# Other banks, another order of subtractions, and accumulating transfers in a hybrid decoder layer

## The chip, the cores and the metric

One core of a Trainium2 chip runs the whole layer. The metric is the device time of one execution in microseconds (us); the median of three runs of the kernel before is 1123.79 us. A difference under 0.2% (some 2.2 us) can hardly be told from none.

## The reference

One decoder layer, 256 tokens of width 2048, all in float32:

```python
h   = RMSNorm_pre(x)
p   = h @ W_in                       # 2048 x 5376
A   = sliding_window_attention(p)    # 16 heads, window 128, ALiBi, sinks
R   = hgrn2_recurrence(p)            # 8 heads of 128, chunkwise
m   = concat[RMSNorm(A), R] @ W_out  # 2048 x 2048
x   = x + RMSNorm_post(m)
u   = relu(RMSNorm_pre2(x) @ W_up)   # 2048 x 8192
x   = x + RMSNorm_post2((u * u) @ W_down)
```

The change lies wholly in the last part, from the residual after `W_out` to the end of `W_up` and `W_down`.

## The kernel before

Every large product is made of three matmuls on float32r operands: a weight tile is cast to a high part `whi` on ScalarE (line 90, or 689), the low part `wlo` is subtracted from it on VectorE (line 91, or 694, `split_weight` or `lo_t`), and activations are split in the same way after a TensorE transpose (`turn_act`, lines 637 to 640, `turn_u`, lines 669 to 674). TensorE then adds high by high, high by low and low by high into a PSUM bank of 128 x 512. All weights stream from HBM once, in tiles of 1 MB (128 partitions x 4 x 512).

From the last part of `W_out` on, the order of TensorE, and from the residual of the first token block on also that of VectorE, ScalarE and SyncE, is the order in which the code is written (two manual schedules). GpSimd is not in them; its instructions stand in the order in which their work comes up.

PSUM banks are taken from tags: `sc` has three, `pj` three, `tr` one and `o` one. A transpose into a tag waits until the bank that it takes over has been read, by ScalarE for the high part and by VectorE for the low part.

**The opening of the MLP** (us 397 to 440 of the span): while TensorE ends the second token block of `W_out` (`w3`), VectorE scales the first block's rows (`scaled(tb, c)`, line 704, writing `hn`), TensorE turns them (`turn(tb, c)`), and the first weight tiles of `W_up` are cast and subtracted: `cast2(i)` makes the high part of tile `i` in two halves, `lo_t(i, h)` the low half `h`, and after the second half of tile `i` it issues the load of tile `i + 3`, since three raw tiles fit (tag `raw`). So `lo_t(0, 1)` lets tile 3 load, and `lo2(1)` (both halves of tile 1) lets tile 4 load. `part(tb, tile, "hh" or "lh" or "hl")` are four matmuls each. `residual(tb)` forms the residual and the row statistics of a token block.

**The chunks.** The 8192 columns go in eight chunks of 1024. Chunk 0 is done plainly; chunks 1 to 7 of `W_up` use Winograd's form of Strassen's scheme, with seven products (`m1` to `m7`) instead of eight on sums of quarter tiles. The sums of activations (`turn_sum`, keys `s1` to `s4`) are made once. Sums of weights are made in every chunk by VectorE (`plus`, `add`, line 873), in place on the raw tiles: `X` (upper left), `P` and `Q` (right), and `R`, the lower left tile, which is loaded into a `P` buffer. Each is two 1 MB halves. `X` becomes in turn X+P, X+P+Q, and X+P+Q+R in the end, which `m4` uses; a further sum waits until the split of the earlier one has read the tile.

A period `ch` runs as a list of segments `q`, in which products of chunk `ch` (12 matmuls each half) alternate with `W_down` products of chunk `ch - 1` (24 matmuls each); the list `plan` says at which segment a weight sum is added, `loads` at which one a load is issued, `turns` at which one activations are turned. For each segment the loop runs the sums (`adds`), the split of the weights two segments ahead (`prepare(k + 2)`, three `whi`/`wlo` buffers), then `turns`, the matmuls, and the loads. In the first period (`ch == 1`), segment 1 first turns the activation sum `s4` in two pieces (`turn_sum`, `c` = 0 and 1) and one piece of chunk 0's `u`, segment 2 another piece of `u` (`t(d, 1, 1, d)`). Two of the three `sc` banks hold `W_down` sums at that time.

Of the kernel before, what the change touches and what calls it, by code (L numbers as in the profile page):

```python
# [12 lines left out]
ALU = mybir.AluOpType  # L13
# [16 lines left out]
def tile_hybrid_layer(  # L30
# [17 lines left out]
    nc = tc.nc  # L48
# [4 lines left out]
    w_up_v = w_up[0].rearrange("(kt p) c -> p kt c", p=P)  # L53
# [17 lines left out]
    def bank(tag, bufs=3):  # L71
        return psum.tile([P, 512], F32, tag=tag, name=nm(tag), bufs=bufs)
# [24 lines left out]
    def load_wide(wv, kt0, c0, pieces=1):  # L97
        return [split_weight(wv[:, kt0 + 4 * i:kt0 + 4 * i + 4, c0:c0 + 512], pieces=pieces) for i in range(4)]
# [216 lines left out]
    for tb in range(2):  # L315
        for par in range(2):
            nc.scalar.activation(out=kz[:, par::2, tb, par * HD:(par + 1) * HD],
                                 in_=kvb[tb][:, 0:P].rearrange("p (n d) -> p n d", n=2), func=AF.Copy,
# [323 lines left out]
    def turn(tb, c):  # L642
        turn_act(hn[tb][:, c * 512:(c + 1) * 512], *(h2T[c][:, :, i, tb * P:(tb + 1) * P] for i in range(2)))

    for c in range(3):
        ch = load_wide(w_out_v, 0, c * 512)
# [19 lines left out]
    def turn_u(uT, cb, tb, u, tag, bufs):  # L666
        tp = bank(tag, bufs)
        for i in range(4):
            nc.tensor.transpose(tp[:, i * P:(i + 1) * P], u[:, i * P:(i + 1) * P], ident)  # L669
        u2 = upool.tile([P, 4, P], F32, tag="u2", name=nm("u2"), bufs=2)  # L670
        nc.scalar.activation(out=u2, in_=tp.rearrange("p (a t) -> p a t", a=4), func=AF.Square)
        hi, lo = (uT[cb][:, :, i, tb * P:(tb + 1) * P] for i in range(2))
        nc.scalar.copy(out=hi, in_=u2)
        nc.vector.tensor_tensor(out=lo, in0=u2, in1=hi.bitcast(F32), op=ALU.subtract)
# [16 lines left out]
    def lo_t(i, h):  # L691
        k = slice(2 * h, 2 * h + 2)
        hi, lo = up_w[i]
        nc.vector.tensor_tensor(out=lo[:, k], in0=up_raw[i][:, k], in1=hi[:, k].bitcast(F32), op=ALU.subtract)
        if h == 1:
            load_t(i + 3)
# [5 lines left out]
    def scaled(tb, c):  # L702
        cs = slice(c * 512, (c + 1) * 512)
        nc.vector.scalar_tensor_tensor(out=hn[tb][:, cs], in0=x2[tb][:, cs], scalar=rh[:, tb:tb + 1], in1=gpre[c],
                                       op0=ALU.mult, op1=ALU.mult)

    ch = load_wide(w_out_v, 0, 3 * 512, pieces=2)
# [18 lines left out]
    def part(tb, tile, kind):  # L726
        for kt in range(4 * tile, 4 * tile + 4):
            a = tok(h2T, kt, tb)[1 if kind == "lh" else 0]
            b = up_w[tile][1 if kind == "hl" else 0][:, kt % 4, :]
            nc.tensor.matmul(ps[tb], lhsT=a, rhs=b, start=kt == 0 and kind == "hh", stop=kt == NKT - 1 and kind == "hl")  # L730

    def cast2(i):
        cast_t(i, 0)
        cast_t(i, 1)

    def lo2(i):
        lo_t(i, 0)
        lo_t(i, 1)


    w3(0, 11)
    scaled(0, 0)
    scaled(0, 1)
    cast2(0)
    turn(0, 0)
    scaled(0, 2)
    w3(11, 13)
    turn(0, 1)
    cast2(1)
    scaled(0, 3)  # L750
    lo_t(0, 0)
    w3(13, 15)
    turn(0, 2)
    w3(15, 16)
    turn(0, 3)
    evac_post(3, 1, banks[1])
    lo_t(0, 1)
    cast2(2)
    uT = new_uT()
    ps += [bank("pj"), bank("pj")]  # L760
# [9 lines left out]
    scaled(1, 1)  # L770
    part(0, 0, "hl")
    part(0, 3, "hh")
    turn(1, 0)
    part(0, 3, "lh")
    scaled(1, 2)
# [3 lines left out]
    turn(1, 2)  # L779
    part(1, 1, "hh")  # L780
    turn(1, 3)
    lo2(1)
    part(1, 2, "hh")
    part(1, 3, "hh")
    for tile_ in range(4):
# [11 lines left out]
    def half(tb, h):  # L797
        return hn[tb][:, h * 1024:(h + 1) * 1024]
# [4 lines left out]
    def turn_sum(src, c, tag="sc", bufs=3):  # L803
        t = sums[src[0]]
        turn_act(src[1][:, c * 512:(c + 1) * 512], *(t(slice(4 * c, 4 * c + 4), i) for i in range(2)), tag, bufs)
# [135 lines left out]
    raws, banks3, us, uTs = {}, {}, {0: prev}, {0: uT}  # L941
# [45 lines left out]
        m1[1].act.append(lambda: copy_out(0, "a", ch))  # L987
        return m1

    def t(ch, cb, tb, dst, tag="sc"):  # L990
        return lambda: turn_u(uTs[dst], cb, tb, us[ch][cb, tb], tag, 3)

    def period(ch, m1_next):
        d = ch - 1
        m5 = [up_seg("X", ch, h, "b", lambda: sums["s1"], True) for h in range(2)]
        m6 = [up_seg("X", ch, h, "a", lambda: sums["s2"], False) for h in range(2)]
        m7 = [up_seg("P", ch, h, "a", lambda: sums["s3"], False) for h in range(2)]
        m3 = [up_seg("Q", ch, h, "b", lambda: sums["s4"], False) for h in range(2)]
        m4 = [up_seg("X", ch, h, "a", lambda: sums["a22"], False) for h in range(2)]
        m2 = [up_seg("R", ch, h, "c", lambda: sums["a12"], True) for h in range(2)]  # L1000
        dn = [[down_seg(d, c, h) for h in range(2)] for c in range(4)]
        if ch == 1:
            q = [None, m1_first[0], m1_first[1], dn[0][1], m5[0], m5[1], dn[1][0], m6[0], m6[1], dn[1][1],
                 m7[0], m7[1], dn[2][0], m3[0], m3[1], dn[2][1], m4[0], m4[1], m2[0], m2[1],
                 m1_next[0], dn[3][0], m1_next[1], dn[3][1]]
        else:
            q = [m5[0], m5[1], dn[0][0], m6[0], m6[1], dn[0][1], m7[0], m7[1], dn[1][0], m3[0], m3[1], dn[1][1],
                 m4[0], m4[1], dn[2][0], m2[0], m2[1], dn[2][1], m1_next[0], dn[3][0], m1_next[1], dn[3][1]]
        A, B, C = ((lambda b=b: banks3[b, ch]) for b in "abc")
        m5[1].act.append(lambda: copy_out(1, "b", ch))  # L1010
        m6[1].act.append(lambda: copy_out(2, "a", ch))
        m7[1].dve.append(comb(ch, (1, 1), ALU.subtract, lambda: scr[1], A))
        m7[1].act.append(relu_in_place(ch, (1, 1)))
        m3[1].dve.append(comb(ch, (1, 0), ALU.subtract, B, lambda: scr[2]))
        m3[1].act.append(relu_in_place(ch, (1, 0)))
        m4[1].act.append(lambda: relu_21(ch))
        m2[1].dve.append(comb(ch, (0, 0), ALU.add, C, lambda: scr[0]))
        m2[1].act.append(relu_in_place(ch, (0, 0)))

        def plus(to, frm, c, h):  # L1020
            return lambda: add(raws[to, c, h], raws[frm, c, h])

        nx = ch + 1


        if ch == 1:
            plan = [(1, "X", "P", ch, 0), (2, "X", "P", ch, 1), (3, "X", "Q", ch, 0), (4, "X", "Q", ch, 1),
                    (6, "P", "Q", ch, 0), (7, "P", "Q", ch, 1), (12, "X", "R", ch, 0), (14, "X", "R", ch, 1),
                    (19, "X", "P", nx, 0), (21, "P", "Q", nx, 0), (22, "X", "P", nx, 1), (23, "X", "Q", nx, 0)]
        else:  # L1030
            plan = [(1, "X", "Q", ch, 1), (2, "P", "Q", ch, 1), (8, "X", "R", ch, 0), (10, "X", "R", ch, 1)]
            if nx < NCH:
                plan += [(17, "X", "P", nx, 0), (19, "P", "Q", nx, 0), (20, "X", "P", nx, 1), (21, "X", "Q", nx, 0)]
        for k, to, frm, c, h in plan:
            q[k].adds.append(plus(to, frm, c, h))
        if ch == 1:
            q[1].turns += [lambda c=c: turn_sum(("s4", half(0, 0)), c) for c in range(2)]
            q[1].turns.append(t(d, 1, 0, d))
            q[2].turns.append(t(d, 1, 1, d))
            loads = [(1, "d", d, 1, 1), (4, "d", d, 2, 0), (7, "d", d, 2, 1),  # L1040
                     (8, "R", ch, 0), (9, "R", ch, 1), (10, "d", d, 3, 0), (11, "Q", nx, 0), (12, "Q", nx, 1),
                     (13, "d", d, 3, 1), (14, "X", nx, 0), (15, "X", nx, 1), (16, "P", nx, 0), (17, "P", nx, 1),
                     (19, "d", ch, 0, 0), (21, "d", ch, 0, 1)]
        else:
            q[0].turns += [t(d, 0, 0, d), t(d, 0, 1, d)]
            q[3].turns.append(t(d, 1, 0, d))
            q[4].turns.append(t(d, 1, 1, d))
            loads = [(0, "d", d, 1, 0), (3, "d", d, 1, 1), (5, "R", ch, 0), (6, "R", ch, 1), (6, "d", d, 2, 0),
                     (9, "d", d, 2, 1), (12, "d", d, 3, 0), (15, "d", d, 3, 1),
                     (17, "d", ch, 0, 0), (19, "d", ch, 0, 1)]  # L1050
            if nx < NCH:
                loads += [(8, "Q", nx, 0), (9, "Q", nx, 1), (11, "X", nx, 0), (12, "X", nx, 1), (14, "P", nx, 0),
                          (15, "P", nx, 1)]
        for k, name, *where in sorted(loads, key=lambda x: (x[0], x[1] == "d")):
            q[k].loads.append(lambda name=name, where=where: (load_down if name == "d" else load_up)(
                *(where if name == "d" else [name] + where)))
        return [x for x in q if x is not None], q
# [10 lines left out]
    for ch in range(1, NCH):  # L1068
        m1 = first_products(ch + 1) if ch < NCH - 1 else [None, None]
        part, q = period(ch, m1)  # L1070
# [96 lines left out]
```

## Time and profile before

| what | before |
|---|---|
| median of 3 runs (lowest, highest) | 1123.79 us (1122.62, 1124.88) |
| the profiled execution, its own time | 1124.23 us |
| its span, first to last instruction | 1122.5 us |
| mean granted TensorE clock | 0.985 |
| busy: TensorE, VectorE, ScalarE, GpSimd | 1088.4, 846.4, 623.0, 19.1 us |
| HBM read over the span | 204.51 MB |

TensorE is busy for 97% of the span, so what can be won at once is the 34 us in which it isn't, and time in which it runs at a lower clock. All times below are us from the first instruction. A row of the timeline gives the start, the busy time, the engine, the line, the operation and what the engine waited for; a row of the chain of work that ended last gives start, time and what ran.

### The profile page before, as it was taken

What the parts mean: (1) busy time and instruction counts of PE and PEld (TensorE: products, weight loads), DVE (VectorE), ACT (ScalarE), POOL (GpSimd) and SP (SyncE); (2) the same over time, 40 slices, a digit from 0 to 9 for tenths busy, and PEclk for the clock granted to TensorE, in tenths of its full rate; (3) what the DMA queues carried; (4) which work ended last, traced back from release to release, by engine and by line L of the source; (5) the groups of instructions that cost most, each with busy time, mean ns of one, the idle gap of its engine ahead of it and who ended that gap; (6) DMA issues with size and microseconds to landing.
All of it is one profiled execution on the core that took longest, in us unless ns stands there. A gap on an engine that the chain in (4) does not pass through costs nothing.

```text
span 1122.5 us, 14032 instructions
## 1 busy us (share of the span) xinstructions
PE 1088.4 (97%) x5708; PEld 928.5 (83%) x5708; DVE 846.4 (75%) x765; ACT 623.0 (55%) x719; POOL 19.1 (2%) x48
## 2 busy tenths in 40 slices
PE   9999999999999989879999999999999999999996
PEld 8999789999988867658788888888888888888885
DVE  6755666665655457578898898898898898898565
ACT  6655655546454353445665565565565575575542
POOL 2100000000000000000000000000000000000000
PEclk9999989999999999979999999999999999999998
DMA  8743414444468635816727727728628628634662
GB/s 278 245 155 121 153 66 151 151 151 152 149 202 319 209 132 184 303 38 215 246 102 268 257 76 273 251 78 279 243 88 280 232 96 282 222 107 156 231 256 75
DMA packets 125538, 209.61 MB, mean 187 GB/s; under 512 B 3945, under 2 KB 49570, under 8 KB 124450
## 3 DMA queue, kind: packets, MB, share of 16 engines
q1 hardware_dynamic: 125474, 208.72, 54.5%
q8 instruction: 45, 0.74, 0.3%
q14 instruction: 19, 0.16, 0.0%
HBM read 204.51 MB, written 4.19 MB: 186 GB/s over the span
## 4 chain that ended last, share of the span: by engine, by line
PE 90%; DVE 3%; DMA 3%; ACT 2%; issue 1%; SPq 0%; POOL 0%; DVEq 0%; POOLq 0%; ACTq 0%
PE pj L869 22%; PE pj L112 10%; PE pj L113 10%; PE pj L111 10%; PE sc L113 8%; PE sc L111 8%; PE sc L112 8%; DVE wlo L91 2%; PE o L112 1%; PE tr L113 1%; PE o L113 1%; PE tr L112 1%; PE tr L111 1%; ACT whi L90 1%; PE o L111 1%; PE sc L669 1%
## 5 line engine op out<-in xcount | busy, mean ns | idle before, releaser
L91 DVE TENSOR_TENSOR wlo<-raw,whi 128x2048 fp32r<-128x2048 f32 (+2 forms) x77 | 145.6, 1901 | 72.5 <-ACT whi L90 71.3
L90 ACT CAST whi<-d 128x2048 fp32r<-128x2048 f32 x59 | 112.9, 1913 | 113.5 <-PE sc L113 78.9
L91 DVE TENSOR_TENSOR wlo<-d,whi 128x2048 fp32r<-128x2048 f32 x59 | 135.1, 2289 | 49.2 <-ACT whi L90 49.2
L90 ACT CAST whi<-raw 128x2048 fp32r<-128x2048 f32 (+2 forms) x77 | 121.8, 1596 | 80.9 <-PE pj L113 33.2
L90 ACT CAST whi<-X 128x2048 fp32r<-128x2048 f32 x56 | 107.2, 1915 | 88.4 <-DVE X L873 31.4
L111 PE MATMUL sc<-whi,uT 128*128 128x512 f32 x384 | 149.5, 389 | 0.0
L113 PE MATMUL sc<-whi,uT 128*128 128x512 f32 x384 | 149.4, 389 | 0.0
L112 PE MATMUL sc<-wlo,uT 128*128 128x512 f32 x384 | 149.4, 389 | 0.0
L869 PE MATMUL pj<-whi,hT 128*128 128x512 f32 x448 | 145.7, 394 | 0.0
L91 DVE TENSOR_TENSOR wlo<-X,whi 128x2048 fp32r<-128x2048 f32 x56 | 127.9, 2284 | 14.2 <-ACT whi L90 14.2
L112 PE MATMUL pj<-hT,whi 128*128 128x256 f32 x384 | 111.4, 290 | 0.0
L113 PE MATMUL pj<-hT,wlo 128*128 128x256 f32 x384 | 110.6, 288 | 0.4 <-DVE wlo L91 0.3
L111 PE MATMUL pj<-hT,whi 128*128 128x256 f32 x384 | 110.5, 288 | 0.4 <-DVE zq L431 0.4
L869 PE MATMUL pj<-whi,a 128*128 128x512 f32 x336 | 109.8, 395 | 0.0
L869 PEld LDWEIGHTS pj<-whi,hT 128*128 128x128 f32 x448 | 85.2, 190 | 17.8
L869 PE MATMUL pj<-wlo,hT 128*128 128x512 f32 x224 | 88.1, 393 | 0.0
L112 PEld LDWEIGHTS sc<-wlo,uT 128*128 128x128 f32 x384 | 72.1, 188 | 15.1
L113 PEld LDWEIGHTS sc<-whi,uT 128*128 128x128 f32 x384 | 72.1, 188 | 14.9
L111 PEld LDWEIGHTS sc<-whi,uT 128*128 128x128 f32 x384 | 72.1, 188 | 14.9
L91 DVE TENSOR_TENSOR wlo<-P,whi 128x2048 fp32r<-128x2048 f32 x32 | 73.3, 2290 | 13.9 <-ACT whi L90 13.9
L111 PEld LDWEIGHTS pj<-hT,whi 128*128 128x128 f32 x384 | 74.2, 193 | 1.1 <-DVE zq L431 0.7
L113 PEld LDWEIGHTS pj<-hT,wlo 128*128 128x128 f32 x384 | 74.3, 193 | 0.8 <-DVE wlo L91 0.8
(268 smaller groups left out, 2050.1 us busy)
## 6 DMA issues: line engine op xcount, KB each, us to landing
d<-in_w_down_dram SPq DMA_DIRECT2D x59, 1024.0 KB, 5.0
P<-in_w_up_dram SPq DMA_DIRECT2D x28, 1024.0 KB, 5.7
raw<-in_w_in_dram SPq DMA_DIRECT2D x24, 1024.0 KB, 5.2
raw<-in_w_in_dram SPq DMA_DIRECT2D x35, 512.0 KB, 4.5
raw<-in_w_out_dram SPq DMA_DIRECT2D x16, 1024.0 KB, 5.1
X<-in_w_up_dram SPq DMA_DIRECT2D x14, 1024.0 KB, 5.4
Q<-in_w_up_dram SPq DMA_DIRECT2D x14, 1024.0 KB, 5.4
raw<-in_w_up_dram SPq DMA_DIRECT2D x8, 1024.0 KB, 5.4
```

Of the source, the lines that this page charges most:

```text
L90: nc.scalar.copy(out=hi[:, k], in_=raw[:, k])
L91: nc.vector.tensor_tensor(out=lo[:, k], in0=raw[:, k], in1=hi[:, k].bitcast(F32), op=ALU.subtract)
L111: nc.tensor.matmul(o, lhsT=ah, rhs=bh, start=first, stop=False)
L112: nc.tensor.matmul(o, lhsT=ah, rhs=bl, start=False, stop=False)
L113: nc.tensor.matmul(o, lhsT=al, rhs=bh, start=False, stop=last)
L669: nc.tensor.transpose(tp[:, i * P:(i + 1) * P], u[:, i * P:(i + 1) * P], ident)
L869: nc.tensor.matmul(o, lhsT=a, rhs=b, start=fresh and kt == 0 and i == 0, stop=kt == 7 and i == 2, skip_group_check=not fresh)
```

## The change

Three edits, all in the written order.

1. In the MLP's opening the four `scaled` of the first token block come first, `lo_t(0, 0)` before the first `turn` and `lo_t(0, 1)` before the second; `lo2(1)` moves from behind the second block's turns to ahead of them.
2. At the first period's opening the two pieces of `s4` turn in the banks `tr` and `o`, and the second piece of `u` in `tr`, instead of all in `sc`.
3. The sums with `R` leave VectorE: in each of seven chunks two transfers, issued by GpSimd, read the lower left quarter from HBM once more and add it to `X` in SBUF as it lands. They are written behind segment 3 or 4 of a period (7 or 8 in the first). `R` itself is loaded as before, since the product `m2` uses it.

```diff
     w3(0, 11)
-    scaled(0, 0)
-    scaled(0, 1)
+    for c in range(4):
+        scaled(0, c)
     cast2(0)
+    lo_t(0, 0)
     turn(0, 0)
-    scaled(0, 2)
+    lo_t(0, 1)
     w3(11, 13)
     turn(0, 1)
     cast2(1)
-    scaled(0, 3)
-    lo_t(0, 0)
...
-    lo_t(0, 1)
...
+    lo2(1)
     turn(1, 0)
...
-    lo2(1)
...
-    def t(ch, cb, tb, dst, tag="sc"):
-        return lambda: turn_u(uTs[dst], cb, tb, us[ch][cb, tb], tag, 3)
+    def t(ch, cb, tb, dst, tag="sc", bufs=3):
+        return lambda: turn_u(uTs[dst], cb, tb, us[ch][cb, tb], tag, bufs)
...
+        def plus_dma(c, h):
+            return lambda: nc.gpsimd.dma_start(out=raws["X", c, h], accum_op=ALU.add,
+                                               in_=w_up_v[:, 8 + 4 * h:12 + 4 * h, c * 1024:c * 1024 + 512])
+
         for k, to, frm, c, h in plan:
-            q[k].adds.append(plus(to, frm, c, h))
+            if frm == "R":
+                q[(7 if ch == 1 else 3) + h].loads.append(plus_dma(c, h))
+            else:
+                q[k].adds.append(plus(to, frm, c, h))
         if ch == 1:
-            q[1].turns += [lambda c=c: turn_sum(("s4", half(0, 0)), c) for c in range(2)]
+            q[1].turns += [lambda c=c: turn_sum(("s4", half(0, 0)), c, ("tr", "o")[c], 1) for c in range(2)]
             q[1].turns.append(t(d, 1, 0, d))
-            q[2].turns.append(t(d, 1, 1, d))
+            q[2].turns.append(t(d, 1, 1, d, "tr", 1))
```

VectorE at the opening of the MLP, kernel before. `hn` are scaled rows, `hT` their turned low parts, `wlo` with `raw_3829` the two halves of tile 0, `rf` the first step of the second block's residual:

```order
L704 SCALAR_TENSOR_TENSOR hn_3857<-x_0_3335,rh,gpre 128x512 x2
L640 TENSOR_TENSOR hT_3352<-sc_3901,hT_3352 128x4x128
L704 SCALAR_TENSOR_TENSOR hn_3857<-x_0_3335,rh,gpre_3344 128x512
L640 TENSOR_TENSOR hT_3353<-sc_3915,hT_3353 128x4x128
L704 SCALAR_TENSOR_TENSOR hn_3857<-x_0_3335,rh,gpre_3345 128x512
L694 TENSOR_TENSOR wlo_3898<-raw_3829,whi_3897 128x1024
L640 TENSOR_TENSOR hT_3354<-sc_3934,hT_3354 128x4x128
L640 TENSOR_TENSOR hT_3355<-sc_3944,hT_3355 128x4x128
L608 TENSOR_TENSOR mg_3342<-pj_3780,gmix 128x512
L694 TENSOR_TENSOR wlo_3898<-raw_3829,whi_3897 128x1024
L599 TENSOR_TENSOR rf_3981<-pss_3350,ppart 128x1
```

The same place in the changed kernel:

```order
L704 SCALAR_TENSOR_TENSOR hn_3857<-x_0_3335,rh,gpre 128x512 x2
L704 SCALAR_TENSOR_TENSOR hn_3857<-x_0_3335,rh,gpre_3344 128x512
L704 SCALAR_TENSOR_TENSOR hn_3857<-x_0_3335,rh,gpre_3345 128x512
L694 TENSOR_TENSOR wlo_3900<-raw_3829,whi_3899 128x1024
L640 TENSOR_TENSOR hT_3352<-sc_3904,hT_3352 128x4x128
L694 TENSOR_TENSOR wlo_3900<-raw_3829,whi_3899 128x1024
L640 TENSOR_TENSOR hT_3353<-sc_3920,hT_3353 128x4x128
L640 TENSOR_TENSOR hT_3354<-sc_3937,hT_3354 128x4x128
L640 TENSOR_TENSOR hT_3355<-sc_3947,hT_3355 128x4x128
L608 TENSOR_TENSOR mg_3342<-pj_3780,gmix 128x512
L599 TENSOR_TENSOR rf_3981<-pss_3350,ppart 128x1
```

The second half of tile 0, which lets tile 3 load, moved ahead of three turned low parts and of `mg`; the residual's first step now follows `mg` at once.

TensorE at the first period's opening, kernel before, from the last `W_down` matmul of chunk 0 on (L637 turns `s4`, L669 turns `u`, L869 is the first product):

```order
L113 MATMUL sc_4329<-whi_4271,uT_3961 128x512
L637 MATMUL sc_4394<-ident,hn_3857 128x128 x4
L637 MATMUL sc_4401<-ident,hn_3857 128x128 x4
L669 MATMUL sc_4408<-ident,u_4381 128x128 x4
L869 MATMUL pj_4417<-whi_4373,hT_3352 128x512
```

The same place in the changed kernel, where the product is line 867:

```order
L113 MATMUL sc_4329<-whi_4271,uT_3961 128x512
L637 MATMUL tr_4394<-ident,hn_3857 128x128 x4
L637 MATMUL o_4401<-ident,hn_3857 128x128 x4
L669 MATMUL sc_4408<-ident,u_4381 128x128 x4
L867 MATMUL pj_4417<-whi_4373,hT_3352 128x512
```

No instruction moved; the first three turns take three different tags, and the fourth (12 matmuls later) takes `tr`.

VectorE in the period of chunk 2, kernel before, around the sums with `R` (here `P_5117` and `P_5137`):

```order
L91 TENSOR_TENSOR wlo_5142<-Q_4664,whi_5141 128x2048
L972 TENSOR_TENSOR u_5157<-scr,pj_4855 128x512
L873 TENSOR_TENSOR X_4737<-X_4737,P_5117 128x2048
L91 TENSOR_TENSOR wlo_5161<-Q_4700,whi_5160 128x2048
L91 TENSOR_TENSOR wlo_5194<-d_5061,whi_5193 128x2048
L873 TENSOR_TENSOR X_4770<-X_4770,P_5137 128x2048
L91 TENSOR_TENSOR wlo_5215<-X_4737,whi_5214 128x2048
```

The same place in the changed kernel:

```order
L91 TENSOR_TENSOR wlo_5144<-Q_4666,whi_5143 128x2048
L970 TENSOR_TENSOR u_5159<-scr,pj_4855 128x512
L91 TENSOR_TENSOR wlo_5162<-Q_4701,whi_5161 128x2048
L91 TENSOR_TENSOR wlo_5195<-d_5062,whi_5194 128x2048
L91 TENSOR_TENSOR wlo_5215<-X_4737,whi_5214 128x2048
```

Two additions are gone here, 14 over the seven chunks; SyncE's order of loads is as before.

## The prediction

> **What bounds the kernel now.** I read the busy shares first (the table above: 1088.4 of 1122.5 us), then who TensorE waited for (us in total, times, longest), then the windows of one whole period of the chunks (length, busy time of TensorE, weight loads, VectorE, ScalarE and GpSimd, TensorE clock, DMA share, GB/s).
>
> ```profile
> PE sc L637 <- DVE hT L640: 11.2, 1, 11.2
> PE pj L730 <- ACT whi L689: 3.7, 2, 3.5
> ...
> PE sc L669 <- DVE hT L640: 1.4, 1, 1.4
> PE pj L112 <- DVE wlo L91: 1.3, 1, 1.3
> ...
> PE o L112 <- DVE wlo L91: 0.7, 1, 0.7
> ...
> 567.00:651.00 84.00, 84.00 (x380) 69.60 (x379) 76.19 (x45) 50.56 (x38) 0.00 (x0) 1.00 0.60 203
> ```
>
> In a period TensorE is busy 84 of 84 us at full clock: VectorE, 76 us busy, holds it up nowhere there. What can be won lies in the named waits, and in the low clock behind the long ones. The first, second, third and fourth rows are at the places that the edits touch.
>
> **Edit 1, the opening.** The chain that ended last and the timeline give this place.
>
> ```profile
> 403.45 1.42 DVE L704 SCALAR_TENSOR_TENSOR hn<-x,rh,gpre 128x512 f32<-128x512 f32 x2 [0.67 <-POOL rh L629]
> ...
> 412.73 0.15 DVE L599 TENSOR_TENSOR rf<-pss,ppart 128x1 f32<-128x1 f32 x1
> ...
> 415.01 1.07 PE L730 MATMUL pj<-wlo,hT 128*128 128x512 f32 x4
> ...
> 416.37 0.63 ACT L589 ACTIVATE junk<-x 128x512 f32<-128x512 f32 x1
> ...
> 418.13 1.41 DVE L704 SCALAR_TENSOR_TENSOR hn<-x,rh,gpre 128x512 f32<-128x512 f32 x2 [0.66 <-POOL rh L629]
> ...
> 426.98 3.28 PE L730 MATMUL pj<-whi,hT 128*128 128x512 f32 x13
> ```
>
> ```profile
> 411.68 1.14 DVE wlo L694
> 412.88 5.54 DMA raw<-in_w_up_dram
> 418.44 2.00 ACT whi L689 x2
> 420.48 1.22 PE pj L730 x2
> ...
> 428.57 2.28 DVE wlo L694 x2
> 430.90 5.33 DMA raw<-in_w_up_dram
> 436.31 1.92 ACT whi L90
> 438.25 2.30 DVE wlo L91
> 440.60 0.50 PE pj L112
> ```
>
> Tile 3 loads when the second half of tile 0 is subtracted (412.8), lands at 418.4, is cast, and TensorE, idle from 416.1, resumes at 419.5. In the new order VectorE runs from 403.45 four scalings (0.71 each, from the pair's row), half a tile (1.14), a turned low part (0.68 by its row below, 0.6 from start to start), the other half: ready near 409.1. The load then lands at 409.2 + 5.5 = 414.7. The next thing that is late is ScalarE, which squares the second block's residual until 417.1 (416.37 + 0.63 and reading the sum). That chain starts with `rf`, which loses the 1.14 of half a tile ahead of it: 1.1 to 1.3 earlier, so the cast begins near 415.9 and TensorE resumes near 417.0: 2.5 earlier, after an idle time of 0.9 instead of 3.5.
>
> The second half of edit 1 puts 2.28 of VectorE ahead of the second block's third scaling. Counted on: the scalings of 418.13 come 1.3 earlier and are done at 418.2, tile 1 at 420.5, first turned part 421.1, third scaling 421.8. TensorE, at 0.9 for four matmuls and 0.45 for a turn at full clock, comes to that third turn at 421.2 and waits 0.6; the fourth isn't late. It is at the matmuls of 426.98 by 423.75: 3.2 won, 0.7 of it from the low clock that the shorter idle avoids. If that clock comes all the same, 2.4; if the third scaling isn't late, 3.8.
>
> Tile 4 then loads at 420.6 instead of 430.90, lands at 426, and is cast when `whi` of tile 0 is free (426.5). VectorE gets to it at 432.0, behind tiles 2 and 3 and two sums of 1.2 each, and is done at 434.3; TensorE wants it at 435.8. The wait of 1.3 at 440.60 goes, with 0.1 of restart: 1.4; at worst half of it stays. The loads behind it start earlier too, one after another on SyncE as before.
>
> **Edit 2, the first period's opening.**
>
> ```profile
> 473.50 0.59 ACT L664 ACTIVATE u<-pj 128x512 f32<-128x512 f32 x1
> 473.62 4.57 DVE L91 TENSOR_TENSOR wlo<-X,whi 128x2048 fp32r<-128x2048 f32 x2 [8.82 <-ACT whi L90]
> ...
> 478.12 2.28 DVE L873 TENSOR_TENSOR X<-X,P 128x2048 f32<-128x2048 f32 x1
> ...
> 482.52 0.68 DVE L640 TENSOR_TENSOR hT<-sc,hT 128x512 fp32r<-128x512 f32 x1
> 483.26 1.12 PE L637 MATMUL sc<-ident,hn 128*128 128x128 f32 x4 [11.16 <-DVE hT L640]
> ...
> 485.77 1.11 PE L669 MATMUL sc<-ident,u 128*128 128x128 f32 x4 [1.40 <-DVE hT L640]
> ...
> 495.02 0.39 PE L111 MATMUL sc<-whi,uT 128*128 128x512 f32 x1
> ...
> 503.50 2.29 DVE L91 TENSOR_TENSOR wlo<-d,whi 128x2048 fp32r<-128x2048 f32 x1
> ...
> 505.90 0.39 PE L111 MATMUL sc<-whi,uT 128*128 128x512 f32 x1
> ```
>
> ```profile
> 419.50:423.70 4.20, 3.95 (x12) 2.95 (x13) 0.54 (x2) 1.52 (x2) 0.00 (x0) 0.59 0.03 12
> ...
> 486.50:491.80 5.30, 5.30 (x14) 4.04 (x13) 2.89 (x2) 1.21 (x2) 0.00 (x0) 0.50 0.09 36
> ```
>
> The second turn waits for the one free `sc` bank, which VectorE reads only at 482.5, behind two splits, a sum and a third split in its order. The third turn then waits once more. In the changed kernel three banks are free: both pieces of `s4` turn by 472.4, `u` when ScalarE has it (474.1), and the first product starts with its high part, going on when the low part is there (473.62 + 2.29 = 475.9); at 0.227 a matmul (48 between 495.02 and 505.90) it ends at 478.5. Then a new wait takes the place of the old: the fourth turn wants `tr`, which VectorE frees at 483.2, with its order unchanged. So TensorE idles 4.8 instead of 11.2 + 1.4 and resumes at the same 483.26, but with one product done: a turn (0.45) and 12 matmuls (2.72) take it to 486.4 at full clock, where it was at 495.02 before. That would be 8.6.
>
> Two things cut it. The clock: behind the 3.5 idle it was 0.59 of full for 4.2 us, a loss of 1.7; behind the 11.2 it was 0.50 until 491.8. An idle of 4.8 is nearest to the first, but broken work lengthened the second: 1.7 to 3.2, the latter 6.4 at half, and I take 2.3. [...] The second is VectorE, whose queue decides: the split at 503.50 ends 0.1 before its matmul wants it. Counted on from 482.52 with 0.6 for a turned part and 2.2 for a sum or a split, that split starts at 482.5 + 4 x 0.6 + 5 x 2.2 = 495.9, which is 7.6 earlier. So the gain lies between 5.4 and 7.5; I take 8.6 - 2.3 = 6.3. ScalarE's casts there wait for `whi` buffers of products that now end earlier.
>
> The wait of 0.7 at 558 stays: that chain starts from a TensorE segment's end, through a `P` load, and moves with it.
>
> **Edit 3, the sums with R.** VectorE loses 14 x 2.28 = 32 us. TensorE has no wait in the periods, so this gains nothing; it loses nothing if the transfers land in time.
>
> ```profile
> X<-in_w_up_dram SPq DMA_DIRECT2D x14, 1024.0 KB, 5.4
> ...
> x<-x_dram SPq DMA_DIRECT2D x2, 1024.0 KB, 8.1
> ```
>
> ```profile
> 580.32 2.28 DVE L91 TENSOR_TENSOR wlo<-X,whi 128x2048 fp32r<-128x2048 f32 x1
> ...
> 584.73 2.29 DVE L91 TENSOR_TENSOR wlo<-X,whi 128x2048 fp32r<-128x2048 f32 x1
> ...
> 609.71 1.92 ACT L90 CAST whi<-X 128x2048 fp32r<-128x2048 f32 x1 [0.81 <-PE pj L869]
> ...
> 611.15 2.28 DVE L873 TENSOR_TENSOR X<-X,P 128x2048 f32<-128x2048 f32 x1
> ...
> 613.54 1.92 ACT L90 CAST whi<-X 128x2048 fp32r<-128x2048 f32 x1 [1.91 <-DVE X L873]
> ```
>
> ```profile
> 582.00:612.00 30.00, 30.00 (x138) 24.82 (x137) 26.81 (x17) 19.55 (x16) 0.00 (x0) 1.00 0.59 205
> ```
>
> `X` is free for the first transfer at 582.6, for the second at 587.0; ScalarE cast the halves at 609.7 and 613.5, the second after waiting, with no TensorE wait behind it. The cover is 27 us each. No accumulating transfer is in this trace. The nearest row is a plain load of the same 1 MB, 5.4; the slowest plain 1 MB of the list is 8.1. Reading the destination as well may double it. Even 2 x 8.1 each, one behind the other, ends at 582.6 + 32.4 = 615.0, 1.5 behind the second cast and within what the split has before TensorE wants it. The DMA engines are 0.59 busy there and the next loads wait many us for their segments, so I cost the edit at 0. GpSimd has nothing else until the end; what queues behind its waits are only the later transfers. Bounds: a gain is excluded by 84 of 84 busy; the loss is the first rival's. [...]
>
> **Sum.** 3.2 + 1.4 + 6.3 = 10.9. The profiled execution took 1124.2, so 1113.3; it stands 0.4 above the median, so I forecast 1112.9. With the ends of the terms (2.4 + 0.7 + 5.4 = 8.5 and 3.8 + 1.4 + 7.5 = 12.7) this case reaches from 1111.1 to 1115.3.
>
> **Rivals.** *The accumulating transfers land too late, and the kernel is slower.* Place: ScalarE's cast of `X` for `m4`, in seven chunks. With a time T each in one queue, the second ends at 582.6 + 2T; from T = 15.5 on, nearly three plain loads, it is behind the cast at 613.5. Seven chunks lose 7 x (2T - 31): the 10.9 are eaten at T = 16.3, and at T = 20 the kernel takes 1113 + 63 = 1176. For it: VectorE is busy 76 of 84 us, and GpSimd must prepare these transfers beside it. Against: 41% of the DMA time there is free. [...] Chance 0.12, most of it well above 1119.
>
> *Half of edit 2 is eaten.* The clock stays at half through the first product too, the fourth turn's new wait is longer, or VectorE's sums come later by one wait for a `whi` buffer: 3 left instead of 6.3, a time near 1116. For it: 9 us at half clock after the old wait. Against: VectorE's order up to 482.5 depends on nothing that TensorE does there. Chance 0.12.
>
> *The opening moves nothing.* The casts of tile 3 wait for the squares, and the second block's turns for tile 1's subtraction, so that 2 of the 4.6 are left: near 1115.5; both edits failing together, 1118.5. Chance 0.08.
>
> *No measurable change*, 0.02: a few of the above, with transfers that delay loads by 1 us per chunk.
>
> **Chances.** Forecast 0.66, the rivals as given. Faster by over 0.2% (2.2 us, what a measurement can tell) 0.86, same 0.02, slower 0.12. The range of 1110.8 to 1118.5 holds the forecast with its bounds and the two partial cases.
>
> **What would show it.** In the changed profile: TensorE's wait at tile 3's cast is about 1 instead of 3.5, none at tile 4; at the first period one wait of 4 to 5 at the turn of `u` into `tr` instead of 11.2 and 1.4; the clock at half for one or two windows behind it; a DMA queue of GpSimd with 14 MB and landings under 15; whole periods still 83.5 long with TensorE full. The forecast is wrong if TensorE waits for line 90's cast of `X` in the periods, or if the period's length grows.

## The result and the profile after

The changed kernel takes 1113.13 us (median; 1112.53 to 1113.56), the kernel before beside it 1123.81 (1122.62 to 1124.88): a ratio of 0.9905 (0.9888 to 0.9922), 10.7 us less. A second set of runs on another chip gave 1113.68 (1112.85 to 1114.45) against 1124.51. The profiled execution took 1112.53 us, its span is 1110.8, the mean granted clock 0.991.

Who TensorE waited for, after (us in total, times, longest):

```profile
PE tr L669 <- DVE hT L640: 4.5, 1, 4.5
...
PE sc L669 <- ACT u L664: 1.6, 1, 1.6
...
PE pj L730 <- ACT whi L689: 1.1, 2, 0.8
...
PE sc L637 <- DVE hn L704: 0.9, 2, 0.7
```

The 11.2 at the turn of `s4`, the 1.4 behind it and the 1.3 at tile 4 are gone, the 3.7 at tile 3 is 1.1. New is one wait of 4.5 at the fourth turn, into `tr`, as forecast, and two shorter ones ahead of it: 1.6 for ScalarE's `u` and 0.9 for the first product's low part. The next fences show where. First the opening, from the timelines of SyncE, ScalarE, TensorE and VectorE:

```profile
408.59 0.37 SPq L78 DMA_DIRECT2D raw<-in_w_up_dram  x1
...
415.31 1.98 ACT L689 CAST whi<-raw 128x1024 fp32r<-128x1024 f32 x2
...
403.73 0.66 PE L637 MATMUL sc<-ident,hn 128*128 128x128 f32 x4 [0.17 <-DVE hn L704]
...
416.39 0.74 PE L730 MATMUL pj<-whi,hT 128*128 128x512 f32 x2 [0.85 <-ACT whi L689]
...
421.52 0.63 PE L637 MATMUL sc<-ident,hn 128*128 128x128 f32 x4 [0.72 <-DVE hn L704]
...
423.26 5.75 PE L730 MATMUL pj<-whi,hT 128*128 128x512 f32 x24
...
431.70 2.28 DVE L91 TENSOR_TENSOR wlo<-raw,whi 128x2048 fp32r<-128x2048 f32 x1
```

Tile 3 is asked for at 408.59, cast from 415.31 on, behind the squares of the residual, and TensorE resumes at 416.39 after 0.85. The third turn of the second block then waits 0.72, which it didn't before. Tile 4 is subtracted at 431.70, before TensorE wants it. Now the first period, TensorE and VectorE, after:

```profile
466.25 0.60 PE L637 MATMUL tr<-ident,hn 128*128 128x128 f32 x4
...
468.89 0.65 PE L669 MATMUL sc<-ident,u 128*128 128x128 f32 x4 [1.61 <-ACT u L664]
...
470.72 0.50 PE L867 MATMUL pj<-wlo,hT 128*128 128x512 f32 x1 [0.94 <-DVE wlo L91]
...
478.01 1.11 PE L669 MATMUL tr<-ident,u 128*128 128x128 f32 x4 [4.49 <-DVE hT L640]
...
483.75 0.40 PE L111 MATMUL sc<-whi,uT 128*128 128x512 f32 x1
...
477.27 0.68 DVE L640 TENSOR_TENSOR hT<-tr,hT 128x512 fp32r<-128x512 f32 x1
```

```profile
417.40:421.50 4.10, 3.41 (x18) 2.53 (x19) 4.10 (x6) 1.17 (x2) 0.00 (x0) 1.00 0.17 63
...
478.00:483.20 5.20, 5.19 (x15) 4.22 (x16) 5.20 (x4) 1.21 (x2) 0.00 (x0) 0.50 0.63 202
...
555.70:639.20 83.50, 83.50 (x378) 69.21 (x377) 71.47 (x42) 50.34 (x37) 2.58 (x2) 1.00 0.72 228
```

Three turns and one product now run while VectorE works through its queue; the fourth turn waits until VectorE frees `tr`. In the second fence (windows: length, busy TensorE, weight loads, VectorE, ScalarE, GpSimd, clock, DMA share, GB/s) the clock stays full behind the 0.85 of the opening; behind the 4.5 it is at 0.50 for 5.2 us. A whole period, the last row, is full for TensorE as before, with VectorE 71.5 us busy.

The same two marks in the timeline before, to measure each part against: the first turn of the opening, and the first turn of `s4`.

```profile
404.26 0.66 PE L637 MATMUL sc<-ident,hn 128*128 128x128 f32 x4 [0.18 <-DVE hn L704]
...
471.50 0.60 PE L637 MATMUL sc<-ident,hn 128*128 128x128 f32 x4
```

Between the marks lie 67.24 us before and 62.52 after: 4.7 for edit 1. From the turn of `s4` to the `W_down` matmul that stood at 495.02 before and stands at 483.75 now lie 23.52 and 17.50: 6.0 for edit 2. That is 10.7 of the 11.7 by which the spans differ; 0.5 arose ahead of the first mark (404.26 against 403.73; in the twelve other profiles of kernels told of below it lies anywhere from 403.45 to 405.99), and 0.4 behind the last (627.5 and 627.05 to the span's end).

The accumulating transfers, after: the queue (packets, MB, share of 16 engines' span) and the group of their issues (median to landing) from the page, then the timelines of GpSimd and ScalarE in chunk 2, then the landings of the first, of the second and of all fourteen.

```profile
q0 software_dynamic: 7392, 14.68, 7.5%
...
X<-in_w_up_dram POOLq DMA_DIRECT2D x14, 1024.0 KB, 10.8
```

```profile
571.60 1.28 POOL L1033 DMA_DIRECT2D X<-in_w_up_dram  x1 [64.50 <-DVE wlo L91]
580.43 1.30 POOL L1033 DMA_DIRECT2D X<-in_w_up_dram  x1 [7.54 <-DMA X<-in_w_up_dram]
...
598.35 1.92 ACT L90 CAST whi<-X 128x2048 fp32r<-128x2048 f32 x1 [0.81 <-PE pj L867]
601.02 1.92 ACT L90 CAST whi<-X 128x2048 fp32r<-128x2048 f32 x1 [0.76 <-PE pj L867]
```

```profile
DMA to landing us min/median/max: 8.5/8.5/8.5
...
DMA to landing us min/median/max: 13.6/13.6/13.6
...
DMA to landing us min/median/max: 8.4/10.8/14.5
```

The first lands at 580.1, the second at 580.43 + 13.6 = 594.0. The casts of 598.35 and 601.02 wait for a `whi` buffer, not for a transfer: 7.0 us are to spare.

### The profile page after: what moved, and what is told of

Read it like the earlier page. It is cut to its first block, busy times and chain, and to the rows that moved or that the text cites. A ratio compares the mean times of both kernels' runs of the same rounds, so it can differ in the third digit from the quotient of the medians.

```text
span 1110.8 us, 14084 instructions
## 1 busy us (share of the span) xinstructions
PE 1084.3 (98%) x5708; PEld 924.8 (83%) x5708; DVE 816.2 (73%) x751; ACT 622.8 (56%) x719; POOL 37.6 (3%) x62
## 3 DMA queue, kind: packets, MB, share of 16 engines
q0 software_dynamic: 7392, 14.68, 7.5%
## 4 chain that ended last, share of the span: by engine, by line
PE 90%; DVE 3%; ACT 2%; issue 1%; DMA 1%; POOL 0%; DVEq 0%; POOLq 0%; ACTq 0%
PE pj L867 22%; PE pj L112 10%; PE pj L113 10%; PE pj L111 10%; PE sc L113 8%; PE sc L111 8%; PE sc L112 8%; PE o L112 1%; PE tr L113 1%; PE o L113 1%; PE tr L112 1%; PE tr L111 1%; PE o L111 1%; PE pj L730 1%; DVE wlo L91 1%
## 6 DMA issues: line engine op xcount, KB each, us to landing
X<-in_w_up_dram POOLq DMA_DIRECT2D x14, 1024.0 KB, 10.8
```

## The experiments

**One edit undone at a time, and edit 3 alone.** Five rounds, one chip; the kernel before stood at 1124.59 there (15 runs). In `no_edit1` the opening has its old order, in `no_edit2` all turns of the first period are in `sc` again, in `no_edit3` `plus` on VectorE makes all the sums:

```diff
 # no_edit1
-    for c in range(4):
-        scaled(0, c)
+    scaled(0, 0)
+    scaled(0, 1)
...
 # no_edit2
-            q[2].turns.append(t(d, 1, 1, d, "tr", 1))
+            q[2].turns.append(t(d, 1, 1, d))
...
 # no_edit3
-            if frm == "R":
-                q[(7 if ch == 1 else 3) + h].loads.append(plus_dma(c, h))
-            else:
-                q[k].adds.append(plus(to, frm, c, h))
+            q[k].adds.append(plus(to, frm, c, h))
```

`only_edit3` is the kernel before with those lines of edit 3 added.

> The changed kernel with edit 1 undone (the opening's order as before). My theory: the three edits win independently, 4.6 here, so this takes 1113.1 + 4.6 = 1117.7 us, with TensorE waits of 3.5 at tile 3's cast and 1.3 at tile 4's subtraction back. Rival (what the opening wins is only waited for later, at the first period): 1113 to 1114.

> The changed kernel with edit 2 undone (all turns of the first period in sc). My theory: 1113.1 + 6.0 to 6.3 = 1119.1 to 1119.4 us, with the waits of 11.2 and 1.4 back. Rival (edit 2 gains nothing without the emptier VectorE queue of edit 3, or the clock eats it): under 1116.

> The changed kernel with edit 3 undone (VectorE adds R itself again, no accumulating transfers). My theory: TensorE waits for VectorE nowhere in the periods, so 1113.1 within 0.5 us. Rival (the 28 additions taken from VectorE do give TensorE time): 1115 or more. Other rival (the transfers cost something): 1112 or less.

> The kernel before with edit 3 alone. My theory: no change, 1123.8 within 0.5 us, with 14 transfers of GpSimd landing in about 10.8 us each and no TensorE wait in the periods. Rival (the transfers delay other loads, or free VectorE where TensorE waits for it): a difference of 1 us or more either way.

(Where an expectation speaks of 28 additions, it is 14, two in each of seven chunks.)

| kernel | median us (lowest, highest) | ratio to before (95%) |
|---|---|---|
| no_edit1 | 1117.88 (1116.40, 1119.66) | 0.9948 (0.9934, 0.9961) |
| no_edit2 | 1118.44 (1116.72, 1119.20) | 0.9945 (0.9932, 0.9957) |
| no_edit3 | 1112.77 (1112.61, 1114.62) | 0.9902 (0.9888, 0.9915) |
| only_edit3 | 1124.69 (1122.82, 1126.62) | 1.0002 (0.9994, 1.0011) |

TensorE's waits in `no_edit1`:

```profile
PE pj L730 <- ACT whi L689: 3.7, 1, 3.7
...
PE pj L112 <- DVE wlo L91: 1.6, 1, 1.6
```

In `no_edit2`:

```profile
PE sc L637 <- DVE hT L640: 11.2, 1, 11.2
...
PE sc L669 <- DVE hT L640: 1.4, 1, 1.4
```

Each edit, undone, brings back its own waits and leaves the other's alone. Between the marks `no_edit1` has 67.45 us against 62.52 with edit 1, so edit 1 is worth 4.7 to 4.9. From the turn of `s4` to the `W_down` matmul `no_edit2` has 22.18, `only_edit3` 23.08 and the kernel before 23.52; the eight profiles here in which the fourth turn goes into `tr` have 16.36 (`no_edit3`) to 17.78 (`ring2816`, below). So edit 2 is worth 5.8 by the means (22.9 less 17.1), and 4.4 to 7.2 by the ends, by how much half clock each profile happens to have there. The time of `no_edit1` is the expected one; that of `no_edit2` is 0.7 below the lower end of what was expected.

The fourth turn in `no_edit3`:

```profile
478.95 1.11 PE L669 MATMUL tr<-ident,u 128*128 128x128 f32 x4 [2.97 <-DVE hT L640]
```

The first product ran at half clock there, from 471.6 to 475.0, so TensorE came to this turn later and waited 3.0 instead of 4.5. The turn itself stands 11.77 us behind the first turn of `s4` (467.18); in `after` it is 11.76 (478.01 less 466.25), in `after_again`, `no_edit1` and `no_tile1_move` 11.77. VectorE's queue sets that time, so half clock ahead of the turn cost nothing here, and half clock behind it did: in `no_edit3` the matmuls behind the turn are back at 0.23 us each from 481.93 on, 3.0 us behind it, in `after` 5.2 us behind it, and the stretch takes 16.36 and 17.50.

Edit 3 alone moves nothing, and taking it away moves nothing either. Its period (windows, `only_edit3`), to be held against the row of the kernel before:

```profile
567.00:651.00 84.00, 84.00 (x380) 69.63 (x379) 71.98 (x43) 50.36 (x38) 2.59 (x2) 1.00 0.72 228
```

VectorE has 72.0 us instead of 76.2, TensorE the same 84 of 84. What edit 3 takes from VectorE held nobody up.

**The second half of edit 1 alone.** Four kernels on one chip, this and the next two with `after_again`, the changed kernel itself, as their base.

```diff
 # no_tile1_move
-    lo2(1)
     turn(1, 0)
...
+    lo2(1)
```

> The changed kernel with the second half of edit 1 undone: the subtraction of tile 1 stands behind the second block's turns again. By the prediction's term: TensorE waits about 1.3 at tile 4's first product again (1.4 lost with its restart), and gains the 0.6 to 0.7 at the third turn of the second block: 0.7 slower, 1113.8. Rival, that the move buys nothing because tile 4 was late only through the first tile's order: 1112.5, or less by the 0.7 of the turn.

> The changed kernel itself beside the three others on the same chip, as their base: 1113.1 as measured before, at most 0.6 off.

`no_tile1_move` took 1113.77 us (1112.99 to 1115.82), `after_again` 1113.68: by the times not to be told apart. In the trace the wait of 1.3 at tile 4 is back and the 0.72 at the third turn gone, and between the marks lie 63.26 us against 62.47: 0.8, where 0.7 was expected. At the first period the 4.5 wait is 2.2 there, since the first product ran at half clock (0.43 us a matmul from 474.32 on, where 0.23 is full) and TensorE came to the turn later. I take the term as borne out by the trace, and as too small for these times.

**What bounds the first period now.** The fourth turn in a bank that nobody has to free:

```diff
 # pj_turn
-            q[2].turns.append(t(d, 1, 1, d, "tr", 1))
+            q[2].turns.append(t(d, 1, 1, d, "pj", 3))
```

> The changed kernel with one thing changed: the fourth turn of `u` goes into a third `pj` bank instead of `tr`, so that nothing of VectorE has to free its bank first. My theory: VectorE's queue of splits and sums bounds this place, so the 4.5 us wait at the turn goes, but most of it comes back at the product that waits for VectorE's split behind it: a gain of 0 to 1.5, 1111.5 to 1113. Rival, the bank is the bound: a gain of 5 to 6 (the wait and the half clock behind it), about 1107.

1112.15 us (1111.86 to 1112.69), 1.5 below `after_again`. TensorE's timeline in `pj_turn`:

```profile
480.55 0.50 PE L113 MATMUL sc<-whi,uT 128*128 128x512 f32 x1 [0.55 <-DVE uT L674]
...
485.55 0.80 PE L113 MATMUL sc<-whi,uT 128*128 128x512 f32 x1 [1.99 <-DVE uT L674]
```

The 4.5 is gone from the turn, and 2.5 of it is back in the product, which waits for the low part of `u` that VectorE turns over behind the same sums and splits. So the queue of VectorE is the bound, not the bank: a gain of 5 to 6 is excluded. The 1.5 itself is not clear of chance. From the first mark to the next product (the first matmul of line 867 on `a`) `pj_turn` takes 84.4 us and the changed kernel 85.5, but `no_edit3`, with the fourth turn in `tr`, takes 84.3, by the place of its half clock.

**Sums out of VectorE's way there.**

```diff
 # early_u
-            plan = [(1, "X", "P", ch, 0), (2, "X", "P", ch, 1), (3, "X", "Q", ch, 0), (4, "X", "Q", ch, 1),
-                    (6, "P", "Q", ch, 0), (7, "P", "Q", ch, 1), ...
+            plan = [(1, "X", "P", ch, 0), (2, "X", "P", ch, 1), (5, "X", "Q", ch, 0), (5, "X", "Q", ch, 1),
+                    (8, "P", "Q", ch, 0), (8, "P", "Q", ch, 1), ...
-            q[1].turns += [lambda c=c: turn_sum(("s4", half(0, 0)), c, ("tr", "o")[c], 1) for c in range(2)]
...
-            q[2].turns.append(t(d, 1, 1, d, "tr", 1))
+            q[1].turns.append(t(d, 1, 1, d, "pj"))
+            q[2].turns += [lambda c=c: turn_sum(("s4", half(0, 0)), c, ("tr", "o")[c], 1) for c in range(2)]
```

> The changed kernel with the fourth turn of `u` moved one segment earlier, into the bank that the projections leave free, the two turns of `s4` moved one segment later, and the four first-period sums X+Q and P+Q moved behind the third split (segments 5 and 8 instead of 3, 4, 6, 7). My theory, that what is left of the wait at the first period (4.5 us at the turn of `u`) is VectorE's order of work and not a bank or the clock: the wait shrinks to about 1, with the low clock behind it mostly gone, so 4 to 5 us less than the changed kernel, 1108 to 1109. Rival, that the sums are only put where the next split wants VectorE: the wait comes back at the splits of the segments behind, and the time is 1112 to 1114.

1110.12 us (1109.56 to 1110.36): 3.6 below `after_again`, a ratio of 0.9871 (0.9856 to 0.9886) to the kernel before, where 4 to 5 was expected. From the first mark to the next product it takes 81.3 us, 4.2 less than the changed kernel, which is more than the half clock there moves (6.8 us of it after, 3.4 here, so 1.7). What TensorE still waits for at this place, `early_u`:

```profile
PE sc L669 <- ACT u L664: 2.5, 1, 2.5
...
PE pj L669 <- ACT u L664: 1.6, 1, 1.6
```

No wait for VectorE is left there; the two for ScalarE's `u` are what the expectation had at "about 1". One more kernel put the turns of `s4` back ahead, to fill the 2.5:

```diff
 # early_u2, against early_u
-            plan = [(1, "X", "P", ch, 0), (2, "X", "P", ch, 1), (5, ...
+            plan = [(2, "X", "P", ch, 0), (2, "X", "P", ch, 1), (5, ...
+            q[1].turns += [lambda c=c: turn_sum(("s4", half(0, 0)), c, ("tr", "o")[c], 1) for c in range(2)]
             q[1].turns.append(t(d, 1, 0, d))
             q[1].turns.append(t(d, 1, 1, d, "pj"))
-            q[2].turns += [lambda c=c: turn_sum(("s4", half(0, 0)), c, ("tr", "o")[c], 1) for c in range(2)]
```

> As early_u, but with the two turns of s4 back in the first segment, ahead of the turns of `u`, and the first sum X+P one segment later, so that VectorE turns over s4 and `u` first. Theory: the 0.9 us of turns then fill the 2.5 us in which TensorE waits for ScalarE's first `u`, and nothing is late behind them: 0.9 less than early_u, 1109.2. Rival: ScalarE's casts of the turned s4 stand ahead of the second `u`, whose wait grows from 1.6 by as much: 1110.1, as early_u.

1109.78 us (1109.48 to 1110.03), on another chip: the two are not told apart, and the 0.9 is not there. Both waits are 1.6 now, so neither mechanism holds, although the time is the rival's. The windows say why, `early_u` first:

```profile
471.50:473.00 1.50, 0.84 (x5) 0.84 (x5) 1.50 (x2) 1.50 (x3) 0.00 (x0) 0.63 0.13 51
473.00:474.50 1.50, 1.50 (x6) 1.21 (x5) 1.50 (x2) 1.47 (x3) 0.00 (x0) 0.50 0.00 0
474.50:476.00 1.50, 1.50 (x7) 1.17 (x6) 1.50 (x1) 1.47 (x3) 0.00 (x0) 0.74 0.00 0
```

```profile
470.00:471.50 1.50, 0.18 (x2) 0.00 (x0) 1.50 (x2) 1.50 (x2) 0.00 (x0) 0.77 0.85 330
...
476.00:477.50 1.50, 1.50 (x5) 1.11 (x5) 1.50 (x3) 0.78 (x2) 0.00 (x0) 0.50 0.37 33
477.50:479.00 1.50, 1.50 (x8) 1.25 (x7) 1.50 (x3) 0.00 (x0) 0.00 (x0) 0.95 0.92 326
```

In windows of 0.5 us the clock reads 1.00 or 0.50 in both traces, before and after, and other values only where it changes (11 of 4464 windows), so a window's share at half clock is twice what its clock lacks to 1. In `early_u` that is 1.1, 1.5 and 0.8, in sum 3.4 us; in `early_u2` 0.7, all of the four windows from 471.5 to 477.5, and 0.15, in sum 6.8. There is less idle time, 3.2 instead of 4.1, and twice as long a stretch of half clock, which eats the 0.9: from the first mark to the `W_down` matmul `early_u` takes 75.8 us, `early_u2` 76.1.

**What an accumulating transfer costs.** Three single runs, to be read by their traces. `acc_twice` issues each transfer twice, so that the sums hold R twice; `plain_gpsimd` leaves `accum_op` out, so that R overwrites X; `ring2816` gives the descriptors of GpSimd's transfers 2816 bytes instead of 2048.

```diff
 # acc_twice
-                q[(7 if ch == 1 else 3) + h].loads.append(plus_dma(c, h))
+                q[(7 if ch == 1 else 3) + h].loads += [plus_dma(c, h), plus_dma(c, h)]
 # plain_gpsimd
-            return lambda: nc.gpsimd.dma_start(out=raws["X", c, h], accum_op=ALU.add,
+            return lambda: nc.gpsimd.dma_start(out=raws["X", c, h],
 # ring2816
-    nc = _bacc.Bacc(..., dynamic_dma_scratch_size=2048)
+    nc = _bacc.Bacc(..., dynamic_dma_scratch_size=2816)
```

> The changed kernel with its 14 GpSimd transfers made plain: R overwrites X instead of being added to it, so part of the sum is left out. If the 10.8 us to landing come from the reading of the destination, the transfers land in 5.4 to 6.5 and the second one of a chunk starts some 4 us after the first; if they come from GpSimd's queue, they stay at 10 or more. The time stays within 1 us of the changed kernel either way.

1112.27 us. The queue and the group of issues in `plain_gpsimd`:

```profile
q0 software_dynamic: 3808, 14.68, 4.1%
...
X<-in_w_up_dram POOLq DMA_DIRECT2D x14, 1024.0 KB, 5.9
```

Landed in 5.9 instead of 10.8, with half the packets and 4.1% instead of 7.5% of the DMA engines: it is the adding that costs, not GpSimd's queue. In chunk 2 the second one starts 4.5 us behind the first (571.47 and 575.99), without waiting for its landing.

> The changed kernel built with 2816 bytes for the descriptors of GpSimd's transfers instead of 2048. If the second transfer of a chunk starts only at the landing of the first (a wait of 7.5 us on GpSimd) because there is no room for its descriptors, it starts about 4 us behind the first now, when VectorE has read the second half of X, and the wait of 7.5 is gone or shorter. If that wait has another cause, it stays. The time stays at 1113.

1113.46 us. GpSimd's timeline in `ring2816`, chunk 2:

```profile
572.55 1.29 POOL L1033 DMA_DIRECT2D X<-in_w_up_dram  x1 [69.32 <-DVE wlo L91]
576.95 1.29 POOL L1033 DMA_DIRECT2D X<-in_w_up_dram  x1 [3.11 <-DVE wlo L91]
```

The second starts 4.4 behind the first, when VectorE has read its half of X, and not at the first one's landing. So with 2048 bytes an accumulating transfer was held back until the one before it had landed (issued 8.8 behind it), and only the size was changed: it was room that it waited for. The plain ones were not held back with 2048 (4.5). The second one lands after another 12.7, so 17.1 us after the first was issued instead of 22.4, which nothing needs.

> The changed kernel with each accumulating transfer issued twice (X becomes P + Q + 2R in the sums, so part of the computation is another). Four transfers stand in line in each chunk instead of two. Theory, that each starts about 8.8 us behind the one before and lands 10.8 after its issue: the last lands near 571.6 + 3 x 8.8 + 10.8 = 609 in chunk 2, where ScalarE casts the second half at 601.0 now, so TensorE waits about 4 to 5 in each of seven chunks: 25 to 50 us slower than the changed kernel, 1140 to 1160. Rival, that the cover of 27 us is only half of what there is (TensorE's queue gives more): under 5 us slower.

1207.33 us, 94 above the changed kernel: the direction was right, the size of 25 to 50 was not. GpSimd's and ScalarE's timelines in `acc_twice`, chunk 2, and the landings of the second, third and fourth:

```profile
586.33 1.28 POOL L1033 DMA_DIRECT2D X<-in_w_up_dram  x1 [50.93 <-DVE wlo L91]
595.05 1.30 POOL L1033 DMA_DIRECT2D X<-in_w_up_dram  x1 [7.43 <-issue]
609.05 1.28 POOL L1033 DMA_DIRECT2D X<-in_w_up_dram  x1 [12.71 <-issue]
622.79 1.29 POOL L1033 DMA_DIRECT2D X<-in_w_up_dram  x1 [12.45 <-DMA X<-in_w_up_dram]
...
622.58 1.90 ACT L90 CAST whi<-X 128x2048 fp32r<-128x2048 f32 x1 [10.35 <-DMA X<-in_w_up_dram]
...
631.36 1.90 ACT L90 CAST whi<-X 128x2048 fp32r<-128x2048 f32 x1 [6.89 <-DMA X<-in_w_up_dram]
```

```profile
DMA to landing us min/median/max: 13.7/13.7/13.7
...
DMA to landing us min/median/max: 13.4/13.4/13.4
...
DMA to landing us min/median/max: 8.5/8.5/8.5
```

The two halves take turns, so the first cast waits for the third transfer and the second for the fourth. I had spaced all four 8.8 apart. That is the spacing of a transfer that runs alone; the two that run beside plain loads take 13.7 and 13.4. The fourth lands 45.0 us after the first is issued, not 37, and from the first transfer of one chunk to that of the next it is 96.66 us (586.33 to 682.99) where it is 83.24 in the changed kernel (571.60 to 654.84): 7 x 13.4 = 94. Of this, 58.7 are waits of TensorE at its products (34.4 for ScalarE's `whi`, 24.3 for VectorE's `wlo`); the rest fits the lower clock behind them, 0.955 on the mean instead of 0.991, which the expectation did not count.

## Why the prediction was right

1113.1 to 1113.7 measured, 1112.9 forecast, 10.7 us won against 10.9. The mechanism was right; that the total meets within 0.2 is in part luck, since the stretch of edit 2 alone varies by 1.4 us between profiles with the same order there. By its steps:

- *The opening's first half, 3.2 with the second block's new wait.* Right to a few tenths. The profile after stands 0.53 us earlier from the first mark on. With that taken off, tile 3's load was forecast for 408.7 (408.59), its cast for 415.4 (415.31), the idle time for 0.9 (0.85, and 0.22 before the next pair), the third turn's wait for 0.6 (0.72), and the matmuls for 423.2 (423.26). The idle time left the clock at full, as the term had it (1.00 from 415.4 to 424.0).
- *Tile 4, 1.4.* Right: no wait there. Undone, 1.3 comes back. The two halves together are 4.6 forecast and 4.7 seen.
- *Edit 2, 8.6 less 2.3 for the clock.* Right: the turn into `tr` stands at 478.01, which is the forecast 483.26 less the 5.25 by which all has moved, to the hundredth, because VectorE's order up to there depends on nothing else. The waits of 1.61 and 0.94 ahead of it are in the forecast's positions (474.1 and 475.9), though not in its 4.8 of idle time. The half clock lasted 5.2 us behind the turn, 2.6 lost instead of 2.3, and the sum is 6.0 in this pair of profiles, 5.8 on the mean of all. That broken work lengthens half clock, with 6.4 us of it as the upper end, was the author's estimate; no run singles that out. What the prediction calls one or two windows of half clock was 6.82 us after. In the traces half clock lasts 3.41 us (behind 3.46 of idle time) and 17.07 before, 3.4 in `early_u` and 6.8 in `early_u2`, and behind the same idle times of 1.6 and 0.9 the clock was full after and at half in `no_edit3`, with the same order on TensorE and VectorE there. In `early_u` it came with no idle time there longer than 2.5.
- *VectorE bounds it.* Right for the fourth turn, shown by `pj_turn`: another bank gave 1.5 by the times, not 5 to 6. Not for the split that the term named as its second limit: it ends at 493.64 (491.35 + 2.29), 1.0 before the matmul that wants it (494.64). What cut the 8.6 was the clock alone.
- *Edit 3, nothing.* Right, shown both ways. In the terms of the first rival, 2T is 594.0 - 571.6 = 22.4, so T = 11.2, where 15.5 is harmful. Two things were off within it: the transfers take 8.5 or 13.6 by what runs beside them, with 10.8 as the median of the two kinds, and they stand in line by the room of 2048 bytes (8.8 apart, 4.4 with 2816), not only by VectorE. That reading the destination may double the time was an estimate. The runs come near it for the engines' time (7.5% against 4.1% for the same bytes, 1.8 times); for the landing they do not, since 8.5 alone is 1.4 times the 5.9 of the plain one.
- *The slower rival.* It didn't come, and its price was sound: 7 x (2T - 31) with the 45.0 of `acc_twice` gives 98 us, measured 94. VectorE's busy time, which stood for it, held up no transfer in a way that a run shows: the landings of 8.4 to 14.5 came with VectorE 71.5 of 83.5 us busy in a period.
- *The partial rivals.* Neither came. Of the first, one condition did occur: in `no_edit3` and `no_tile1_move` the first product ran at half clock, which only shortened the wait behind it (2.97 and 2.23 instead of 4.49). The split at 491.35 lost 0.46 to a wait for `whi`, which its 1.0 to spare covers. Of the second, tile 3's cast did wait for the squares, as counted.

## What to carry to other kernels

When a bank is taken away as the bound, count on along the engine that frees it: here its queue gave the end of the new wait to a few hundredths (11.76 or 11.77 us behind the first turn), while its length (2.2 to 4.5) went by TensorE's clock ahead of it. Moving that engine's own work (3.6 us more here) was worth more than a further bank (1.5 by the times, not clear of chance). Work taken from an engine that no one waits for in that stage (here 30 us of VectorE: 846.4 busy before, 816.2 after) was worth nothing there (`only_edit3`: a ratio of 1.0002). The cost of idle time on TensorE did not go by its length alone: 3.2 us of it came with 6.8 of half clock in `early_u2`, 4.1 with 3.4 in `early_u`, and the stretch took 76.1 and 75.8. So less of it can cost as much, and a microsecond of difference behind an idle is no evidence for an order of work.

## What the hardware showed

- An accumulating transfer of 1 MB landed in 8.4 to 8.8 us where hardly anything else ran, and in 12.8 to 14.5 beside plain loads (all fourteen of the changed kernel); a plain one from the same queue took 5.9, in half the packets (3808 against 7392 for 14).
- With 2048 bytes for descriptors the second accumulating transfer was not issued until the first had landed (8.8 us later); with 2816 it came after 4.4. Two plain transfers of the same size came 4.5 apart with 2048.
- Around two idle times of 1.6 us, with a turn of 0.7 between them, the clock went to half for 6.8 us; around idles of 2.5 and 1.6 in nearly the same place for 3.4. Around idles of 1.6 and 0.9 it stayed full in `after`, `after_again` and `no_edit1` and went to half in `no_edit3`, `no_tile1_move` and `pj_turn`, with the same order of work up to there. The 0.85 and 0.72 of the opening left it at full (1.00).
- Half clock came in lengths of 3.41 and 17.07 us before and 6.82 after in this part of the kernel, one, five and two times 3.41; in `early_u` it was 3.4, in `early_u2` 6.8.
